# A two-layer audio trunk on one core: the last convolution block moved in front of the first scores, two casts moved behind key and query 1, and the norm weights' load moved to another queue

## The chip, the cores and the metric

One core of one Trainium2 chip. The time is device microseconds of one execution of the whole program; the comparison is between the median of several executions of the kernel before and of the changed kernel.

## What is computed

```python
for i in range(DEPTH):                                   # DEPTH = 2, 512 tokens, width 1024
    h = h + 0.5 * swiglu(rmsnorm(h, ffn1_norm[i]), ffn1_w_gu[i], ffn1_w_down[i])
    u = rmsnorm(h, mix_norm[i])
    b_g, c_g, v_c, q_c, kv_c, k_r, g_conv, g_mla = jnp.split(u @ w_in[i], split_pts, axis=-1)
    y_conv = short_conv_branch(b_g, c_g, v_c, conv_w[i], w_conv_out[i])
    y_mla = mla_branch(q_c, kv_c, k_r, q_norm[i], kv_norm[i], w_uq[i], w_ukv[i], w_mla_out[i], cos, sin)
    h = h + (sigmoid(g_conv) * y_conv + sigmoid(g_mla) * y_mla) @ w_o[i]
    h = h + 0.5 * swiglu(rmsnorm(h, ffn2_norm[i]), ffn2_w_gu[i], ffn2_w_down[i])
    h = h + sigmoid(rmsnorm(h, ple_norm[i]) @ w_ple_gate[i]) * (p[i] @ w_ple_proj[i])
return rmsnorm(h, final_norm)
```

`mla_branch` is attention with 8 heads. The queries of a head are 128 plain dimensions plus 64 that are turned by the token's position (rotary), keys likewise with one turned key shared by all heads; the mask is causal by chunks of 64 tokens.

## The kernel before

Everything is held transposed: a tile is 128 features by 512 tokens. All products are made in a 32-bit format of TensorE (fp32r) that keeps fewer bits, so every operand is cut into a high and a low part: ScalarE writes the high part (`split`: a copy with a cast, L204; for weights L70), VectorE the rest (a subtraction, L205; for weights L71), and a product of two operands is three matmuls, high times high, high times low, low times high (`mm3`, L212 to L214). Names that end in h and l are these parts.

Weights arrive in "halves" of eight 128 x 128 tiles, one DMA of 512 KB each on SyncE's queue, in the order in which the code asks for them (`Stream.get`). The cut weights `wh`, `wl` lie in 4 buffers each; a fifth cut can only start when the matmuls that read one of the four are done. TensorE's results go to a pool of 8 PSUM banks (`PS`): a new result needs a bank whose last reader is done.

The order of instructions on each engine is set when the program is built, by a scheduler that looks at the code's order and at its own estimates. Each engine then works through its list strictly in that order; an instruction that waits holds up all behind it on that engine.

The change lies in `mixer(l)`, which runs once per layer, and in the load of `cols`, the table of all norm weights. The stages of `mixer` that matter:

- The gates: products of seven parts each (`Sevens.step`, L427, 24 matmuls each); between them stand the blocks of the convolution's output, `conv_out(m)` for m = 0 to 7, each 12 matmuls of 512 columns, and one VectorE product with a gate (L650), which frees its bank. Nothing reads these products before the merge at the mixer's end.
- `qkv(pr)` for the four pairs of heads pr = 0 to 3: the turned queries of both heads (`q_rope`, bank `qr`), then `key(0)`, `query(0)`, `key(1)`, `query(1)` (banks `kn`, `qn`) and `values` (two banks `v`), each with its own cast into two parts; where `values` stands among them depends on how the weights fall into halves. `q_rope_parts` makes from the turned query (rope: `qrt`) one tile for each head (`qr0`, `qr1` below: ScalarE L701, VectorE L702), which the last two matmuls of each score block read.
- `scores(pr, t, ...)` for the heads t = 0, 1 of the pair: four blocks `s<pr><t>p`, one for each 128 queries, of 5 matmuls each over 256, 256, 384 and 512 keys; then VectorE's maximum (L741) and ScalarE's exponential (L743). `turn` transposes them (`t<pr><t>t`, cast into `pth`, `ptl`), and `mix_v` multiplies by the values (`o<pr><t>av`).
- The loop: `qkv(0)`, scores of both heads of pair 0, then for each pair `qkv` of the next, and twice: turn a head of this pair, scores of a head of the next, `mix_v`.

So the names `m0s10p` or `m0h1v` are: layer 0, pair 1, head 0, score block; layer 0, pair 1, values.

Of the kernel before, what the change touches and what calls it, by code (L numbers as in the profile page):

```python
# [9 lines left out]
F32 = mybir.dt.float32  # L10
F32R = mybir.dt.float32r
I32 = mybir.dt.int32
AF = mybir.ActivationFunctionType
ALU = mybir.AluOpType
# [158 lines left out]
def trunk_kernel(ctx, tc, dims, x, p, positions, gains, rope_c, weights, out):  # L173

    nc = tc.nc
    S, D, DEPTH, PD, DFF, CONV, QL, KL = dims
    KD = D // P
# [12 lines left out]
    def G(name, dt=F32):  # L190
        return gp.tile([P, S], dt, tag="g", name=name)

    def PS(name):
        return mp.tile([P, 512], F32, tag="mm", name=name)


    def split(src, name, scale=None):
        hi, lo = G(name + "h", F32R), G(name + "l", F32R)
        split_to(hi, lo, src, scale)
        return hi, lo  # L200

    def split_to(hi, lo, src, scale=None):
        if scale is None:
            nc.scalar.copy(hi, src)  # L204
            nc.vector.tensor_tensor(lo, src, hi.bitcast(F32), ALU.subtract)  # L205
        else:
            nc.scalar.activation(hi, src, AF.Copy, scale=scale)
            nc.vector.scalar_tensor_tensor(lo, src, scale, hi.bitcast(F32), ALU.mult, ALU.subtract)
# [7 lines left out]
    def proj(tiles, vs, name, ps=None):  # L216
        ps = PS(name) if ps is None else ps
        o = ps[:, :vs[0][0].shape[1]]
        for k, (t, v) in enumerate(zip(tiles, vs)):
            mm3(o, W.get(t), v, k == 0, k == len(tiles) - 1)  # L220
        return ps
# [19 lines left out]
    ones = cp.tile([P, P], F32R, tag="ones", name="ones")  # L241
    nc.vector.memset(ones.bitcast(F32), 1.0)
    cols = cp.tile([P, gains.shape[1]], F32, tag="cols", name="cols")
    nc.gpsimd.dma_start(out=cols, in_=gains)
    ident = cp.tile([P, P], F32, tag="ident", name="ident")
    make_identity(nc, ident)
    eps_t = cp.tile([P, 1], F32, tag="eps", name="eps_t")
# [301 lines left out]
    def rope(src, cos, sin, name):  # L549

        t1, t2 = G(name + "t1"), G(name + "t2")
        for a in range(0, P, 64):
            for o, i in ((a, a + 32), (a + 32, a)):
                nc.scalar.copy(t2[o:o + 32, :], src[i:i + 32, :])
        nc.vector.tensor_tensor(t1, src, cos, ALU.mult)
        nc.vector.tensor_tensor(t2, t2, sin, ALU.mult)
        nc.vector.tensor_tensor(t1, t1, t2, ALU.add)
        return t1

    def mixer(l):  # L560
# [32 lines left out]
        for k, (vh, vl) in enumerate(xs):  # L593
            if k % 4 == 0:
                wa, wb = W.halves_of(*kr_cols[k:k + 4])
            t = slice(k % 4 * P, (k % 4 + 1) * P)
# [18 lines left out]
        for k in range(CONV // P):  # L615
            ps = proj(W.col("w_in", l, o_c + k * P, D), xs, f"{name}Cp{k}")
            c = G(f"{name}c{k}")
            nc.vector.tensor_tensor(c, ps, r2, ALU.mult)
            ps = proj(W.col("w_in", l, o_v + k * P, D), xs, f"{name}Vp{k}")
# [7 lines left out]
            ps = proj(W.col("w_in", l, o_b + k * P, D), xs, f"{name}Bp{k}")  # L627
# [20 lines left out]
        def conv_out(m):  # L648
            ps = proj(W.col("w_conv_out", l, m * P, CONV), yc, f"{name}cop{m}")
            nc.vector.tensor_tensor(gates[m], ps, gates[m], ALU.mult)  # L650
# [4 lines left out]
            step(0, j)  # L655
        n_last = KD // 2 - 1
        for n in range(n_last):
            between = [(lambda m=m: conv_out(m)) for m in range(4 * n - 4, 4 * n)] if n else []
            order = [(n + 1, 1), (n, 7), (n + 1, 5), (n, 4)]
            order += [(n + 1, j) for j in ((6, 2, 7, 3, 4) if n + 1 == n_last else (2, 6, 3))]  # L660
            for i, (n_, j_) in enumerate(order):
                step(n_, j_)
                if i in (1, 2, 3, 4 if n + 1 == n_last else 5) and between:
                    between.pop(0)()
                if (n_, j_) == (n_last, 7):
                    qc = [split(t, f"{name}qn{k}") for k, t in enumerate(qt)]
                    kvc = [split(t, f"{name}kvn{k}") for k, t in enumerate(kvt)]
                    krh, krl = split(krt, name + "kr")
# [3 lines left out]
        def qkv(pr):  # L672
            n = f"{name}h{pr}"
            heads = (2 * pr, 2 * pr + 1)
            res = {}
            def values():
                vw = [W.get(*(("w_ukv", l, k * P, hd * 256 + NOPE) for hd in heads)) for k in range(KL // P)]
                vs = []
                for tb in range(0, NT, 2):
                    ps = PS(f"{n}v{tb}")  # L680
                    for b in range(2):
                        tok = slice((tb + b) * P, (tb + b + 1) * P)
                        o = ps[:, b * 256:(b + 1) * 256]
                        for k, (vh, vl) in enumerate(vw):
                            ch, cl = kvc[k][0][:, tok], kvc[k][1][:, tok]
                            nc.tensor.matmul(o, ch, vh, start=k == 0, stop=False)
                            nc.tensor.matmul(o, ch, vl, start=False, stop=False)
                            nc.tensor.matmul(o, cl, vh, start=False, stop=k == len(vw) - 1)
                    vs.append(split(ps, f"{n}v{tb}"))
                res["v"] = vs  # L690

            def q_rope():
                ps = proj(W.col("w_uq", l, tuple(hd * (NOPE + ROPE) + NOPE for hd in heads), QL), qc, n + "qr")
                res["qr"] = rope(ps, cosT, sinT, n + "qr")

            def q_rope_parts():
                qr = res["qr"]
                for t in range(2):
                    q2 = G(f"{n}qr{t}", F32R)
                    own, oth = slice(t * 64, t * 64 + 64), slice(64 - t * 64, 128 - t * 64)  # L700
                    nc.scalar.copy(q2[own, :], qr[own, :])  # L701
                    nc.vector.tensor_tensor(q2[oth, :], qr[own, :], q2[own, :].bitcast(F32), ALU.subtract)  # L702
                    res["qr", t] = q2

            def key(t):
                ps = proj(W.col("w_ukv", l, heads[t] * 256, KL), kvc, f"{n}kn{t}")
                res["kn", t] = split(ps, f"{n}kn{t}")

            def query(t):
                ps = proj(W.col("w_uq", l, heads[t] * (NOPE + ROPE), QL), qc, f"{n}qn{t}")  # L710
                res["qn", t] = split(ps, f"{n}qn{t}")

            query0 = lambda: query(0)
            parts = [(3, q_rope), (2, lambda: key(0)), (3, query0), (2, lambda: key(1)), (3, lambda: query(1))]
            at = [i for i in range(1, len(parts) + 1) if W.pairs_fit(2, sum(w for w, _ in parts[:i]))]
            parts.insert(at[-1], (4, values))
            for _, part in parts:
                part()
                if part is query0:
                    q_rope_parts()  # L720
            return res

        def scores(pr, t, qk):
            n = f"{name}s{pr}{t}"
            e = [G(f"{n}e{i}") for i in range(3)]
            e = [e[0][:, :P], e[1][:, :2 * P], e[0][:, P:], e[2]]
            sm = ep.tile([P, 16], F32, tag="sm", name=n + "sm")
            (qh, ql), (kh, kl), q2 = qk["qn", t], qk["kn", t], qk["qr", t]
            for i in range(NT):
                q = slice(i * P, (i + 1) * P)  # L730
                n_ = max(2, i + 1) * P
                ps = PS(f"{n}p{i}")
                o = ps[:, :n_]
                nc.tensor.matmul(o, qh[:, q], kh[:, :n_], start=True, stop=False)
                nc.tensor.matmul(o, qh[:, q], kl[:, :n_], start=False, stop=False)
                nc.tensor.matmul(o, ql[:, q], kh[:, :n_], start=False, stop=False)
                nc.tensor.matmul(o, q2[:, q], krh[:, :n_], start=False, stop=False)
                nc.tensor.matmul(o, q2[:, q], krl[:, :n_], start=False, stop=True)
                w = (i + 1) * P
                nc.vector.memset(ps[0:CHUNK, w - CHUNK:w], -1e30)  # L740
                nc.vector.tensor_reduce(sm[:, i:i + 1], ps[:, :w], axis=AX.X, op=ALU.max, negate=True)  # L741
                eo = e[i]
                nc.scalar.activation(eo, ps[:, :w], AF.Exp, bias=sm[:, i:i + 1], accum_out=sm[:, 8 + i:9 + i])  # L743
                nc.vector.reciprocal(sm[:, 12 + i:13 + i], sm[:, 8 + i:9 + i])
                (nc.vector if i % 2 else nc.gpsimd).tensor_scalar(eo, eo, sm[:, 12 + i:13 + i], None, ALU.mult)
            return e
# [31 lines left out]
        pt_h, pt_l = turned_tiles(name)  # L778
        heads = []
        qk = qkv(0)  # L780
        es = [scores(0, t, qk) for t in range(2)]
        NP = N_HEADS // 2
        for pr in range(NP):
# [12 lines left out]
        for m in range(KD):  # L796
            mla_part(m, N_HEADS - 2 if m < 3 else 0, N_HEADS)
            t = m_b[m]
# [3 lines left out]
        for m in range(KD):  # L802
            ps = proj(W.col("w_o", l, m * P, D), merged, f"{name}wop{m}")
# [206 lines left out]
```

## Time and profile before

| | us |
|---|---|
| three timed executions | 2289.72, 2289.80, 2291.17 (median 2289.8) |
| the profiled execution | 2290.97 |
| its span, first to last instruction | 2289.1 |
| TensorE busy in it | 2276.7 (99%) |
| VectorE, ScalarE, GpSimd busy | 1796.1, 1161.2, 34.7 |

Times in the rows of the timeline count from the span's start. A row of it has the start, the duration, the engine (an engine's name with a q is its queue, which issues DMAs), the line, the operation, what it writes and reads, shapes, and in brackets how long the engine sat idle before it and what ended that. Matmuls overlap: the distance between the starts of two is what one costs. Layer 1 repeats layer 0 in every stage spoken of here: its score stretches have the same lengths to 0.02 us.

### The profile page before, as it was taken

The page shows a single profiled execution, that of the slowest core. Times are in us where ns is not written, and L with a number is a line of the kernel's source. Part 1 is how long each engine was busy: PE and PEld are TensorE (multiplying, and loading weights), DVE is VectorE, ACT ScalarE, POOL GpSimd, SP SyncE. Part 2 cuts the span into 40 slices and gives each one's busy share as a digit, 9 for nine tenths or more (in the row PEclk, how much of TensorE's full clock was granted, in tenths as well). Part 3 has the DMA queues.
Part 4 walks back from the last instruction along what each step waited for, and adds up shares of the span by engine and source line. Part 5 has one row for each costly group of instructions (what it writes and reads, how often), then busy time and mean ns, then how long its engine had stood idle before and what let it go on. Part 6 is the DMA issues. An engine that isn't in the chain of part 4 may idle for free.

```text
span 2289.1 us, 34697 instructions
## 1 busy us (share of the span) xinstructions
PE 2276.7 (99%) x14168; PEld 2060.7 (90%) x14168; DVE 1796.1 (78%) x2508; ACT 1161.2 (51%) x1744; POOL 34.7 (2%) x43
## 2 busy tenths in 40 slices
PE   9999999999999999999999999999999999999998
PEld 8999988899888999998899999888988889999988
DVE  8887778877876988877798887768878669877765
ACT  7444445455743644444664444445467356444455
POOL 0000000000200000000000000000001000000000
PEclk9999999999999999999999999999999999999999
DMA  5333343134122233233223333322331123333321
GB/s 194 111 111 93 105 130 102 56 110 138 38 65 85 73 111 111 93 119 122 91 83 94 110 98 115 120 90 67 119 104 56 65 74 102 104 100 99 113 83 38
DMA packets 62975, 222.76 MB, mean 97 GB/s; under 512 B 7120, under 2 KB 7120, under 8 KB 62816
## 3 DMA queue, kind: packets, MB, share of 16 engines
q1 hardware_dynamic: 62208, 219.70, 30.4%
q8 instruction: 111, 1.82, 0.3%
q10 hardware_dynamic: 576, 0.79, 0.1%
q14 instruction: 48, 0.39, 0.1%
q0 software_dynamic: 32, 0.05, 0.0%
HBM read 218.42 MB, written 2.10 MB: 96 GB/s over the span
## 4 chain that ended last, share of the span: by engine, by line
PE 97%; DVE 2%; ACT 0%; issue 0%; DMA 0%; ACTq 0%; POOLq 0%
PE a0pd L212 2%; PE b0pd L212 2%; PE a1pd L212 2%; PE b1pd L212 2%; PE b1pd L213 2%; PE a1pd L213 2%; PE b0pd L213 2%; PE a0pd L213 2%; PE b1pd L214 2%; PE a1pd L214 2%; PE a0pd L214 2%; PE b0pd L214 2%; PE e1gp L212 1%; PE e1gp L214 1%; PE e1gp L213 1%; PE m0mop L212 1%
## 5 line engine op out<-in xcount | busy, mean ns | idle before, releaser
L70 ACT CAST wh<-st 128x1024 fp32r<-128x1024 f32 (+1 forms) x455 | 474.7, 1044 | 574.8 <-issue 57.7
L71 DVE TENSOR_TENSOR wl<-st,wh 128x1024 fp32r<-128x1024 f32 (+1 forms) x456 | 552.4, 1212 | 160.3 <-ACT wh L70 159.5
L70 ACT CAST wh<-s 128x1024 fp32r<-128x1024 f32 x94 | 98.8, 1051 | 132.6 <-PE b1pd L213 8.5
L71 DVE TENSOR_TENSOR wl<-s,wh 128x1024 fp32r<-128x1024 f32 x94 | 114.5, 1218 | 15.6 <-ACT wh L70 15.6
L149 DVE TENSOR_TENSOR st<-st,s 128x1024 f32<-128x1024 f32 x47 | 57.5, 1223 | 1.1
L146 DVE TENSOR_TENSOR s<-s,st 128x1024 f32<-128x1024 f32 x47 | 57.3, 1220 | 0.2
L141 DVE TENSOR_TENSOR s<-st,st 128x1024 f32<-128x1024 f32 x47 | 57.3, 1218 | 0.1
L152 DVE TENSOR_TENSOR st<-st,st 128x1024 f32<-128x1024 f32 x47 | 57.2, 1218 | 0.0
L511 DVE SCALAR_TENSOR_TENSOR h<-b0pd,h 128x512 f32<-128x512 f32 x40 | 27.5, 689 | 9.4 <-PE b0pd L214 9.2
L511 DVE SCALAR_TENSOR_TENSOR h<-b1pd,h 128x512 f32<-128x512 f32 x40 | 27.5, 688 | 9.4 <-PE b1pd L214 9.2
L511 DVE SCALAR_TENSOR_TENSOR h<-a1pd,h 128x512 f32<-128x512 f32 x40 | 27.5, 688 | 7.7 <-PE a1pd L214 7.7
L511 DVE SCALAR_TENSOR_TENSOR h<-a0pd,h 128x512 f32<-128x512 f32 x40 | 27.5, 687 | 6.4 <-PE a0pd L214 6.4
L106 POOL MEMSET wh<- 128x256 f32 x4 | 1.1, 313 | 1191.5 <-DVE wl L71 1191.5
L799 DVE TENSOR_TENSOR m1g<-m1mop,m1g 128x512 f32<-128x512 f32 x8 | 5.5, 690 | 6.5 <-PE m1mop L214 6.5
L799 DVE TENSOR_TENSOR m0g<-m0mop,m0g 128x512 f32<-128x512 f32 x8 | 5.5, 690 | 6.5 <-PE m0mop L214 6.5
L295 ACT ACT_TABLE_LOAD x8 | 10.3, 1283 | 0.1
L910 ACT ACTIVATE fsq<-h 128x256 f32<-128x256 f32 (+1 forms) x10 | 4.8, 480 | 9.9 <-DVE h L891 9.9
L804 DVE TENSOR_TENSOR h<-m0wop,h 128x512 f32<-128x512 f32 x8 | 5.5, 691 | 4.1 <-PE m0wop L214 4.1
L804 DVE TENSOR_TENSOR h<-m1wop,h 128x512 f32<-128x512 f32 x8 | 5.5, 690 | 4.1 <-PE m1wop L214 4.1
L621 DVE TENSOR_TENSOR m0z<-m0Vp,m0c 128x512 f32<-128x512 f32 x4 | 2.8, 692 | 6.2 <-PE m0Vp L214 6.2
L621 DVE TENSOR_TENSOR m1z<-m1Vp,m1c 128x512 f32<-128x512 f32 x4 | 2.8, 691 | 6.2 <-PE m1Vp L214 6.2
L650 DVE TENSOR_TENSOR m0g<-m0cop,m0g 128x512 f32<-128x512 f32 x8 | 5.5, 688 | 2.5 <-PE m0cop L214 2.5
(11171 smaller groups left out, 8787.5 us busy)
## 6 DMA issues: line engine op xcount, KB each, us to landing
st<-in_weights SPq DMA_DIRECT2D x406, 512.0 KB, 3.5
h<-in_x SPq DMA_DIRECT2D x8, 256.0 KB, 5.4
st<-in_weights SPq DMA_DIRECT2D x7, 256.0 KB, 5.3
out<-fo SPq DMA_DIRECT2D x7, 256.0 KB, 2.5
e0pi<-in_p SPq DMA_DIRECT2D x2, 256.0 KB, 3.7
e1pi<-in_p SPq DMA_DIRECT2D x2, 256.0 KB, 4.0
st<-in_weights ACTq DMA_DIRECT2D x1, 256.0 KB, 3.7
pos_i<-in_positions ACTq DMA_DIRECT2D x1, 256.0 KB, 3.8
```

The lines of the kernel that those rows point to most:

```text
L70: self.nc.scalar.copy(hi[:, w], src[:, w])
L71: self.nc.vector.tensor_tensor(lo[:, w], src[:, w], hi[:, w].bitcast(F32), ALU.subtract)
L141: tt(self.s, self.a21, self.a22, ALU.add)
L146: tt(self.s, self.s, self.a11, ALU.subtract)
L149: tt(self.a12, self.a12, self.s, ALU.subtract)
L152: tt(self.a11, self.a11, self.a21, ALU.subtract)
L212: nc.tensor.matmul(ps, wh, vh, start=first, stop=False)
L213: nc.tensor.matmul(ps, wh, vl, start=False, stop=False)
L214: nc.tensor.matmul(ps, wl, vh, start=False, stop=last)
L511: nc.vector.scalar_tensor_tensor(h[m], ps, 0.5, h[m], ALU.mult, ALU.add)
L799: nc.vector.tensor_tensor(t, mla_ps[m], t, ALU.mult)
L804: nc.vector.tensor_tensor(h[m], ps, h[m], ALU.add)
```

## The change

Three edits. The load of `cols` is issued by SyncE, as the first entry of its queue, and no longer by GpSimd. In `mixer`, `conv_out(7)` is no longer made between two steps of the gates, but after `qkv(0)` and ahead of the first scores. In `qkv`, `q_rope_parts` for both heads and the casts of the values come after all other parts, in that order.

```diff
-    nc.gpsimd.dma_start(out=cols, in_=gains)
+    nc.sync.dma_start(out=cols, in_=gains)
...
-            between = [(lambda m=m: conv_out(m)) for m in range(4 * n - 4, 4 * n)] if n else []
+            between = [(lambda m=m: conv_out(m)) for m in range(4 * n - 4, min(4 * n, KD - 1))] if n else []
...
-                    vs.append(split(ps, f"{n}v{tb}"))
+                    vs.append(ps)
                 res["v"] = vs
...
-            query0 = lambda: query(0)
-            parts = [(3, q_rope), (2, lambda: key(0)), (3, query0), (2, lambda: key(1)), (3, lambda: query(1))]
+            parts = [(3, q_rope), (2, lambda: key(0)), (3, lambda: query(0)), (2, lambda: key(1)), (3, lambda: query(1))]
             at = [i for i in range(1, len(parts) + 1) if W.pairs_fit(2, sum(w for w, _ in parts[:i]))]
             parts.insert(at[-1], (4, values))
             for _, part in parts:
                 part()
-                if part is query0:
-                    q_rope_parts()
+            for t in range(2):
+                q_rope_parts(t)
+            res["v"] = [split(ps, f"{n}v{2 * i}") for i, ps in enumerate(res["v"])]
             return res
...
         qk = qkv(0)
+        conv_out(KD - 1)
         es = [scores(0, t, qk) for t in range(2)]
```

`q_rope_parts(t)` now makes the tile of one head; its two instructions are unchanged (now L700 and L701).

What this does to the engines' lists. First pair, VectorE, from the first key's low part to the first maximum. Before:

```order
L205 TENSOR_TENSOR m0h0kn0l<-m0h0kn_5506,m0h0kn0h 128x512
L205 TENSOR_TENSOR m0h0qn0l<-m0h0qn_5517,m0h0qn0h 128x512
L71 TENSOR_TENSOR wl_6036<-st_6033,wh_6035 128x1024
L702 TENSOR_TENSOR m0h0qr_5531<-m0h0qrt_5497,m0h0qr_5531 64x512
L702 TENSOR_TENSOR m0h0qr_5534<-m0h0qrt_5497,m0h0qr_5534 64x512
L205 TENSOR_TENSOR m0h0kn1l<-m0h0kn_5537,m0h0kn1h 128x512
L205 TENSOR_TENSOR m0h0v0l<-m0h0v_5554,m0h0v0h 128x512
L205 TENSOR_TENSOR m0h0v2l<-m0h0v_5571,m0h0v2h 128x512
L205 TENSOR_TENSOR m0h0qn1l<-m0h0qn_5588,m0h0qn1h 128x512
L740 MEMSET m0s00p_5612 64x64
```

and in the changed kernel:

```order
L205 TENSOR_TENSOR m0h0kn0l<-m0h0kn_5486,m0h0kn0h 128x512
L205 TENSOR_TENSOR m0h0qn0l<-m0h0qn_5503,m0h0qn0h 128x512
L205 TENSOR_TENSOR m0h0kn1l<-m0h0kn_5517,m0h0kn1h 128x512
L205 TENSOR_TENSOR m0h0qn1l<-m0h0qn_5528,m0h0qn1h 128x512
L650 TENSOR_TENSOR m0g_4842<-m0cop_5588,m0g_4842 128x512
L71 TENSOR_TENSOR wl_6036<-st_6033,wh_6035 128x1024
L701 TENSOR_TENSOR m0h0qr_5574<-m0h0qrt_5477,m0h0qr_5574 64x512
L701 TENSOR_TENSOR m0h0qr_5577<-m0h0qrt_5477,m0h0qr_5577 64x512
L205 TENSOR_TENSOR m0h0v0l<-m0h0v_5548,m0h0v0h 128x512
L205 TENSOR_TENSOR m0h0v2l<-m0h0v_5561,m0h0v2h 128x512
L739 MEMSET m0s00p_5612 64x64
```

Key and query 1 moved up past a weight cut and the turned query; the moved block's gate product (L650) is new here. On TensorE the 12 matmuls of `conv_out(7)` now stand between the values and the first score block.

Second pair, ScalarE. Before:

```order
L701 CAST m0h1qr_5754<-m0h1qrt_5714 64x512
L701 CAST m0h1qr_5757<-m0h1qrt_5714 64x512
L204 CAST m0h1kn1h<-m0h1kn_5760 128x512
L70 CAST wh_6327<-st_6325 128x1024
L204 CAST m0h1qn1h<-m0h1qn_5771 128x512
```

and in the changed kernel:

```order
L204 CAST m0h1kn1h<-m0h1kn_5754 128x512
L204 CAST m0h1qn1h<-m0h1qn_5765 128x512
L70 CAST wh_6327<-st_6325 128x1024
L700 CAST m0h1qr_5811<-m0h1qrt_5714 64x512
L700 CAST m0h1qr_5814<-m0h1qrt_5714 64x512
L204 CAST m0h1v0h<-m0h1v_5785 128x512
```

The cut of the next weights (L70) stood behind the turned query's parts and now stands ahead of them; VectorE's list has the same order (its L71 for these weights directly ahead of L701).

Third pair, ScalarE; here `values` stand ahead of `query(1)`. Before:

```order
L701 CAST m0h2qr_6049<-m0h2qrt_6009 64x512
L701 CAST m0h2qr_6052<-m0h2qrt_6009 64x512
L204 CAST m0h2kn1h<-m0h2kn_6055 128x512
L70 CAST wh_6626<-st_6624 128x1024
L204 CAST m0h2v0h<-m0h2v_6066 128x512
L204 CAST m0h2v2h<-m0h2v_6083 128x512
L204 CAST m0pth_5473<-m0t10t_6120 128x512
L204 CAST m0h2qn1h<-m0h2qn_6100 128x512
```

and in the changed kernel:

```order
L204 CAST m0h2kn1h<-m0h2kn_6049 128x512
L70 CAST wh_6626<-st_6624 128x1024
L204 CAST m0h2qn1h<-m0h2qn_6086 128x512
L204 CAST m0pth_5459<-m0t10t_6120 128x512
L700 CAST m0h2qr_6106<-m0h2qrt_6009 64x512
L700 CAST m0h2qr_6109<-m0h2qrt_6009 64x512
L204 CAST m0h2v0h<-m0h2v_6060 128x512
```

The turned query's parts and the values' casts moved behind query 1 and behind the first transposed block (`pth`).

The banks follow the lists. In the first pair the score blocks take, in turn, the banks of `qr`, `kn0`, `qn0`, `kn1`, `qn1`, of the moved convolution block and of the two `v`; the next pair's `qr` takes that of the first score block. In the second pair the blocks of `s10` take those of `kn1`, `qn1` and the two `v`, before and after. In the third pair they took those of `kn1`, the two `v` and the first transposed block; now those of `kn1`, `qn1`, the first transposed block and the first `v`.

More of the change, by code (lines that the diff above doesn't have):

```diff
@@ L694, in q_rope, with q_rope_parts @@
                 res["qr"] = rope(ps, cosT, sinT, n + "qr")
-            def q_rope_parts():
+            def q_rope_parts(t):
                 qr = res["qr"]
[L698 to L703, printed above, removed]
+                q2 = G(f"{n}qr{t}", F32R)
+                own, oth = slice(t * 64, t * 64 + 64), slice(64 - t * 64, 128 - t * 64)
+                nc.scalar.copy(q2[own, :], qr[own, :])
+                nc.vector.tensor_tensor(q2[oth, :], qr[own, :], q2[own, :].bitcast(F32), ALU.subtract)
+                res["qr", t] = q2
             def key(t):
```

## The prediction

> **What bounds it now.** I read the page's busy times and chain first.
>
> ```profile
> PE 2276.7 (99%) x14168; PEld 2060.7 (90%) x14168; DVE 1796.1 (78%) x2508; ACT 1161.2 (51%) x1744; POOL 34.7 (2%) x43
> PE 97%; DVE 2%; ACT 0%; issue 0%; DMA 0%; ACTq 0%; POOLq 0%
> ```
>
> TensorE is the bound almost everywhere: of the span of 2289.1 us it is idle for 2289.1 - 2276.7 = 12.4. The change removes no matmul, so it can only move time in which TensorE waits. Where those waits are, the view of waits (TensorE's own) says: who waited, for whom, total, times, longest.
>
> ```profile
> PE a0pg L230 <- ACT a0x0h L207: 1.6, 1, 1.6
> PE m0s10p L734 <- DVE m0h1qn1l L205: 0.9, 1, 0.9
> PE m1s10p L734 <- DVE m1h1qn1l L205: 0.9, 1, 0.9
> ```
>
> One wait is at the start, and one in each layer in the scores of the second pair. Waits shorter than a matmul's own overlap are missed by this list, so I measured the score stages by windows of TensorE: from the first score matmul to the first matmul after the stage. The columns are the stretch, its length, TensorE's busy time, its granted clock, DMA share and GB/s. Both heads of pair 0; then head 0 of pair 1, of pair 2, head 1 of pair 2, head 0 of pair 3.
>
> ```profile
> 566.61:574.76 8.15, 7.84 (x41) 1.00 0.41 131
> 587.72:592.26 4.54, 3.67 (x21) 1.00 0.38 115
> 613.57:616.88 3.31, 3.31 (x24) 1.00 0.54 163
> 619.84:623.14 3.30, 3.30 (x24) 1.00 0.00 0
> 637.84:641.13 3.29, 3.29 (x23) 1.00 0.52 159
> ```
>
> A head that waits for nothing costs 3.29. Its 20 matmuls have 5 x (256 + 256 + 384 + 512) = 7040 columns, 0.467 ns each, so 0.12 us for a matmul of 256 columns, 0.18 for 384, 0.24 for 512. The first pair loses 8.15 - 2 x 3.29 = 1.57, the second pair's first head 4.54 - 3.29 = 1.25, the third and fourth pair nothing. Two layers: 2 x (1.57 + 1.25) = 5.6 us is all that the mixer edits can win.
>
> **The norm weights' queue.** The timeline's first microseconds, and from the DMA view the one issue of `h` at 0.73 with its time to landing:
>
> ```profile
> 0.73 0.38 SPq L53 DMA_DIRECT2D h<-in_x  x1
> 1.16 0.42 SPq L51 DMA_DIRECT2D st<-in_weights  x1
> 1.24 0.71 POOL L244 DMA_DIRECT2D cols<-in_gains  x1 [0.81 <-POOLq L999]
> 4.44 0.43 DVE L68 CAST wh<-st 128x512 fp32r<-128x512 f32 x1 [3.44 <-DMA st<-in_weights]
> 5.62 0.72 ACT L207 ACTIVATE a0x0h<-h,cols 128x512 fp32r<-128x512 f32 x1 [2.96 <-DMA cols<-in_gains]
> 6.40 0.80 PE L230 MATMUL a0pg<-a0x0h,wh 128*128 128x512 f32 x1 [1.57 <-ACT a0x0h L207]
> h<-in_x SPq DMA_DIRECT2D x1, 256.0 KB, 3.5
> 8.70 0.63 PE L232 MATMUL a0pu<-a0x0h,wl 128*128 128x512 f32 x1
> 9.12 0.53 PE L232 MATMUL a0pg<-a0x0h,wl 128*128 128x512 f32 x1
> 9.49 0.39 PE L232 MATMUL a0pu<-a0x0h,wl 128*128 128x512 f32 x1
> 9.71 0.39 PE L234 MATMUL a0pg<-a0x0l,wh 128*128 128x512 f32 x1
> ```
>
> ScalarE's first cast waits for `cols`, landed at 5.6, while `h` landed at 0.73 + 3.5 = 4.2. With `cols` first on SyncE, `h` takes the slot at 1.16, 0.43 later, and lands at about 4.7; every later issue of SyncE moves back by as much. No row shows 53 KB on this queue; 256 KB took 3.5, so I take `cols` as landed by 0.73 + 3.5 = 4.2. The cast then starts at 4.7 instead of 5.6, and the first product at about 5.5: 0.9 earlier. Bounds: nothing won, if `h` comes as late as `cols` did, and 1.4 (5.6 - 4.2), if the extra entry costs `h` nothing. The weights are ready (VectorE's cast ends at 4.87). The other tiles of x and weights may land 0.43 later, but the first tile keeps TensorE busy for 12 products of 0.22 to 0.42, so they are not missed. What 0.9 is worth depends on the clock: products start 0.42 apart up to 9.12 and 0.22 apart from 9.49 on, half speed at first. If the step stays at that moment, the 0.9 is won at half speed, 0.45; if it comes earlier with the work, 0.9. I take 0.7. GpSimd loses a DMA that nothing else of the start needs. The scheduler also swaps some neighbours in layer 0's first feed-forward; the wait list has nothing there, so I take 0.
>
> [...]
>
> **The first pair.** Rows of TensorE, ScalarE and VectorE:
>
> ```profile
> 554.79 0.40 PE L212 MATMUL m0h0qr<-m0qn0h,wh 128*128 128x512 f32 x1
> 559.77 0.73 ACT L646 ACTIVATE m0g<-m0g3t 128x256 f32<-128x256 f32 x2 [2.58 <-DVE m0g3t L641]
> 560.52 2.35 ACT L554 COPY m0h0qrt<-m0h0qr 32x512 f32<-32x512 f32 x4
> 565.84 0.68 DVE L205 TENSOR_TENSOR m0h0kn0l<-m0h0kn,m0h0kn0h 128x512 fp32r<-128x512 f32 x1
> 566.44 0.68 DVE L205 TENSOR_TENSOR m0h0qn0l<-m0h0qn,m0h0qn0h 128x512 fp32r<-128x512 f32 x1
> 567.04 1.23 DVE L71 TENSOR_TENSOR wl<-st,wh 128x1024 fp32r<-128x1024 f32 x1
> 568.29 1.40 DVE L702 TENSOR_TENSOR m0h0qr<-m0h0qrt,m0h0qr 64x512 fp32r<-64x512 f32 x2
> 572.21 0.19 DVE L740 MEMSET m0s00p<- 64x64 f32 x2
> 572.73 1.28 ACT L743 ACT_TABLE_LOAD   x1 [2.49 <-DVE m0s00sm L741]
> 574.02 0.37 ACT L743 ACTIVATE m0s00e<-m0s00p,m0s00sm 128x128 f32<-128x128 f32 x1
> ```
>
> A low part costs VectorE 0.60, a weight cut about 1.2, the two turned tiles 1.40. The convolution block, 12 x 0.23 = 2.8 of TensorE, is only moved: the gates' end comes 2.8 sooner, and the scores start when they did. What it gives is time for the casts. The casts themselves also move. The half that `conv_out(6)` opened now serves `q_rope` and key 0's first tile, so the weight cut that needs its buffer waits for the 12th product after the gates, 554.79 + 12 x 0.23 = 557.6 on the old time line (on which the scores would now start 2.7 later, at 569.3). Behind that cut (1.05, and 1.2 on VectorE) stand the turned key's low part 0.6, the last gate's product 0.7 and sigmoids 0.73, and the four copies for the turned query, 2.35: these end near 564.3, where they ended at 562.9. VectorE follows with three operations of the rotation (1.8), a cut (1.2), four low parts (2.4) and the convolution's product (0.6): 570.3, which is 1.0 after the scores' start, called zero from here. The next weight cut waits for the convolution block's third tile of four (its buffer) and is through ScalarE at 0.6, so VectorE does it next, to 2.2; the turned tiles are ready at 2.9 and 3.6, the values at 4.9. TensorE's first 18 matmuls (head 0 whole, two blocks of head 1, without turned tiles) need 2.7, so it waits some 0.2 for the first turned tile and would be through at 6.9. The next product, pair 1's `qr`, needs the bank of score block 0: maximum from 4.9, table load 0.52 after it as in the rows, exponential 1.29 after that, 0.37 long, and its read-out: 7.2. So 7.2 instead of 8.15, a gain of 0.95 per layer. Bounds: 0, and 1.57.
>
> **The second pair.**
>
> ```profile
> 583.62 0.28 PE L686 MATMUL m0h1v<-wh,m0kvn0h 128*128 128x256 f32 x1
> 586.34 1.05 ACT L70 CAST wh<-st 128x1024 fp32r<-128x1024 f32 x1
> 587.58 1.22 DVE L71 TENSOR_TENSOR wl<-st,wh 128x1024 fp32r<-128x1024 f32 x1
> 588.71 0.68 DVE L205 TENSOR_TENSOR m0h1qn1l<-m0h1qn,m0h1qn1h 128x512 fp32r<-128x512 f32 x1
> ```
>
> Count from the values' first matmul, V. Before, score block 0 starts at V + 4.1 and block 1 waits for its bank, that of query 1, whose low part stands behind the weight cut: to V + 5.8 (the wait of 0.9). That wait goes: query 1's low part is now ahead of the cut. What is late next is the cut itself: its buffer is read by the values' products to their end, V + 2.7 (586.34), on both engines, and the turned query now stands behind it. ScalarE's cut ends at V + 3.8, VectorE's 1.1 later at V + 4.9, the first turned tile at V + 5.6, the second at 6.3, the first value at 7.1. TensorE has six matmuls without them (0.7), stands at V + 4.9 until 5.7, does four (0.5), stands at 6.2 until the first value frees the bank of block 2 at 7.1, and needs 0.9 + 1.2 more: V + 9.2. Before it was 592.26 - 583.62 = 8.64. A loss of 0.55; bounds: a gain of 1.25, and a loss of 1.5 (both stands doubled).
>
> **The third pair**, whose values come ahead of query 1:
>
> ```profile
> 610.69 1.06 ACT L70 CAST wh<-st 128x1024 fp32r<-128x1024 f32 x1 [0.26 <-PE m0h2v L688]
> 612.57 0.49 PE L753 MATMUL m0t10t<-ident,m0s10e 128*128 128x128 f32 x3
> 613.68 0.59 ACT L204 CAST m0h2qn1h<-m0h2qn 128x512 fp32r<-128x512 f32 x1
> 616.40 0.18 DVE L740 MEMSET m0s20p<- 64x64 f32 x2
> ```
>
> Count from Q = 612.57, where query 1 is done; the scores start at Q + 1.0 and now lose nothing. After the change both turned tiles and both values wait behind query 1 in both lists. ScalarE: query 1 from Q + 0.2, first transposed block (0.6), turned tiles 0.6 each, done at 1.8 and 2.4. VectorE: query 1 at Q + 1.5, transposed block 2.1, turned tiles 2.8 and 3.5, first value 4.2. TensorE: nine matmuls without turned tiles (1.3), waiting 0.3 for banks, then for the turned tile to Q + 2.9; six more, 0.9; then block 3 needs the first value's bank, Q + 4.3, and 1.2: Q + 5.5 instead of 4.3. A loss of 1.2. Behind it VectorE reaches the maxima 2.2 late (Q + 6.0 for 3.8), TensorE only 1.2: block 1 of head 1 needs the bank of head 0's block 2, whose exponential is late by the difference less its slack: another 0.5. Bounds: 0, and 2.2 (all of VectorE's delay).
>
> **The fourth pair** again has query 1 ahead of the values, so query 1 is done 24 x 0.12 + 1.0 = 3.9 before the scores and not 1.0; by the same count the first value's low part ends about 0.6 before block 2 wants its bank: 0.
>
> **The sum.** A layer: -0.95 + 0.55 + 1.2 + 0.5 = +1.3; two layers +2.6; the start -0.7: +1.9. On the profiled execution's 2290.97 that is 2292.9. That execution lies 1.2 above the median of the runs, 2289.8; on the median it is 2291.7, a change of 0.08%. A change below 0.2% (4.6 us) is about what a measurement of this kernel cannot tell from none.
>
> **Rivals.**
> - [...] Chance 0.15.
> - The casts behind cost nothing: the cover holds in the first pair and later pairs stay as they were. 2289.8 - 2 x 0.95 - 0.7 = 2287.2. For it: VectorE idles in parts of every pair. Chance 0.21.
> - All score waits go: 2289.8 - 5.6 - 0.9 = 2283.3, faster. Against it: the cut that waits for the values stands ahead. Chance 0.05.
> - The backlog reaches the fourth pair too, where it pays like the third (1.7): 2291.7 + 2 x 1.7 = 2295.1, slower. It decides when the first value's low part of pair 3 ends over 0.6 later than my count, behind block 2's start. Chance 0.06.
> - The load does not come sooner, `h` queued behind small rows of `cols`: 2291.7 + 0.7 = 2292.4. Chance 0.04.
>
> My own forecast keeps 0.49, with 2290 to 2293.5 from the halved and full value of the start and half the spread of the pairs' bounds. The range, 2287.0 to 2294.2, takes in all but the two ends, 0.11, and some tail of the others. Faster 0.05, same 0.88, slower 0.07.
>
> **What would show it.** Right: the first product near 5.5; both first heads in about 7.2; the wait for query 1 in the second pair gone and replaced by two stands of about 0.9 before a matmul that reads `qr` and before one that reuses a value's bank; head 0 of pair 2 at 4.5 instead of 3.3. Wrong: if that last stretch is still 3.3, or if pair 3's is not. A start that does not move would show ScalarE's first cast waiting for `h` near 5.6.

## The result, and the profile after

The changed kernel takes 2295.01 us in the median of 16 executions (2291.69 to 2295.49), the kernel before 2290.55 beside it (16 executions, 2289.67 to 2292.67). The ratio is 1.0016, with a 95% interval of 1.0008 to 1.0023. That is slower, by less than the 0.2% that the prediction called no change, and above the upper end of its range, 2294.2.

The executions of the changed kernel fall into three groups: two at 2291.7 to 2291.9, five at 2293.3 to 2293.6, nine at 2294.9 to 2295.5, some 1.7 apart. The profiled execution, 2291.93 with a span of 2289.9, is one of the first group, so its trace shows less than what the median lost. Its busy times differ little from before:

```profile
PE 2275.3 (99%) x14168; PEld 2059.0 (90%) x14168; DVE 1798.5 (79%) x2508; ACT 1161.3 (51%) x1744; POOL 33.1 (1%) x42
```

TensorE now idles 2289.9 - 2275.3 = 14.6 us where it idled 12.4. Its waits (total, times, longest):

```profile
PE a0pg L230 <- ACT a0x0h L207: 1.4, 1, 1.4
PE m0s10p L736 <- DVE m0h1qr L701: 1.0, 1, 1.0
PE m0s10p L733 <- DVE m0h1v0l L205: 0.8, 1, 0.8
PE m0s20p L733 <- DVE m0h2v0l L205: 0.3, 1, 0.3
```

The wait for query 1 is gone; in its place stand one for the turned query and one for the bank that the first value holds, and the third pair has got a wait. The score stretches that the prediction measured, in the same order (stretch, length, TensorE busy, granted clock, DMA share, GB/s):

```profile
564.35:571.47 7.12, 6.87 (x41) 1.00 0.25 94
584.33:589.89 5.56, 3.81 (x23) 1.00 0.30 94
611.20:615.77 4.57, 4.22 (x23) 1.00 0.38 118
618.71:622.36 3.65, 3.64 (x23) 1.00 0.00 0
637.06:640.41 3.35, 3.35 (x23) 1.00 0.36 135
```

Against 8.15, 4.54, 3.31, 3.30 and 3.29: -1.03, +1.02, +1.26, +0.35, +0.06. The whole loss of a layer can be read from its first score to a product far behind; first the row of before, then that of the changed kernel:

```profile
805.10 0.40 PE L212 MATMUL b0pd<-b0a0h,wh 128*128 128x512 f32 x1
```

```profile
804.38 0.40 PE L212 MATMUL b0pd<-b0a0h,wh 128*128 128x512 f32 x1
```

805.10 - 566.61 = 238.49, 804.38 - 564.35 = 240.03: 1.54 lost in each layer, 3.1 in both. At the start, the two loads have changed places, and `h` ends the wait of ScalarE's first cast:

```profile
0.72 0.39 SPq L244 DMA_DIRECT2D cols<-in_gains  x1
1.16 0.42 SPq L53 DMA_DIRECT2D h<-in_x  x1
5.11 0.72 ACT L207 ACTIVATE a0x0h<-h,cols 128x512 fp32r<-128x512 f32 x1 [2.45 <-DMA h<-in_x]
5.88 0.50 PE L230 MATMUL a0pg<-a0x0h,wh 128*128 128x512 f32 x1 [1.41 <-ACT a0x0h L207]
```

So every wait that the prediction named is there, and none of them explains the third group of executions. Two theories for it, both on the clock that TensorE is granted (at 0.50, in the repeated run below, products of 512 columns start 0.42 apart instead of 0.23): A, the two stands of the second pair lie so close that the clock falls to half behind them, in some executions; B, the clock steps up later at the start than it did.

### The profile page after: what moved, and what is told of

Same layout as the page of the kernel before. It is cut to its first block, busy times and chain, and to the rows that moved or that the text cites. A ratio compares the mean times of both kernels' runs of the same rounds, so it can differ in the third digit from the quotient of the medians.

```text
span 2289.9 us, 34697 instructions
## 1 busy us (share of the span) xinstructions
PE 2275.3 (99%) x14168; PEld 2059.0 (90%) x14168; DVE 1798.5 (79%) x2508; ACT 1161.3 (51%) x1744; POOL 33.1 (1%) x42
## 4 chain that ended last, share of the span: by engine, by line
PE 96%; DVE 2%; ACT 1%; issue 0%; DMA 0%; SPq 0%; ACTq 0%
PE b0pd L212 2%; PE b1pd L212 2%; PE a0pd L212 2%; PE a1pd L212 2%; PE a1pd L213 2%; PE a0pd L213 2%; PE b1pd L213 2%; PE b0pd L213 2%; PE b0pd L214 2%; PE a1pd L214 2%; PE b1pd L214 2%; PE a0pd L214 2%; PE e1gp L212 1%; PE e1gp L214 1%; PE e1gp L213 1%; PE m0mop L212 1%
## 5 line engine op out<-in xcount | busy, mean ns | idle before, releaser
L70 ACT CAST wh<-st 128x1024 fp32r<-128x1024 f32 (+1 forms) x455 | 474.7, 1044 | 576.0 <-issue 58.2
L71 DVE TENSOR_TENSOR wl<-st,wh 128x1024 fp32r<-128x1024 f32 (+1 forms) x456 | 552.8, 1213 | 162.0 <-ACT wh L70 161.0
L70 ACT CAST wh<-s 128x1024 fp32r<-128x1024 f32 x94 | 98.8, 1051 | 130.9 <-PE a1pd L213 8.5
L71 DVE TENSOR_TENSOR wl<-s,wh 128x1024 fp32r<-128x1024 f32 x94 | 114.6, 1219 | 14.1 <-ACT wh L70 14.1
```

Of the source, the lines that this page charges most:

```text
L70: self.nc.scalar.copy(hi[:, w], src[:, w])
L71: self.nc.vector.tensor_tensor(lo[:, w], src[:, w], hi[:, w].bitcast(F32), ALU.subtract)
```

## The experiments

Each ratio below is to the kernel before, executed beside the run; its median there was 2289.8 to 2291.3.

**The changed kernel again**, profiled anew, no edit.

> The changed kernel once more, for the spread of its times and for the clock in a second profile. Its profile so far shows waits that cost each layer 1.54 us, 3.1 in all, and a start 2.3 us quicker than in the profile of before; yet its times mostly lie 4 to 5.5 above before's lower times (2289.8). Theory A (the stands drop the clock): in most executions the two stands of 0.95 and 0.8 us in the second pair let the clock fall to half for some microseconds, once per layer, 1.7 us each; then times lie near 2291.8, 2293.5 and 2295.3, and a profile of a 2293.5 or 2295.3 execution shows a granted clock below 1 near 587 or 1720 us. Theory B (the start): the clock steps up later at the start in most executions; such a profile shows the step near 7.4 or 10.8 us and a full clock afterwards. Both expect a median of 2293.5 to 2295.5.

2293.72 (2291.85 to 2295.55), ratio 1.0013 (1.0004 to 1.0022). This profile is of an execution of the third group, 2294.75. Its windows of TensorE (second column length, third busy, then the granted clock), and its timeline at the place:

```profile
586.28:589.69 3.41, 1.67 (x11) 1.00 0.49 148
589.69:593.10 3.41, 3.41 (x11) 0.50 0.04 11
```

```profile
587.62 0.39 PE L736 MATMUL m0s10p<-m0krh,m0h1qr 128*128 128x256 f32 x1 [0.95 <-DVE m0h1qr L701]
589.15 0.41 PE L733 MATMUL m0s10p<-m0h1kn0h,m0h1qn0h 128*128 128x384 f32 x1 [0.79 <-DVE m0h1v0l L205]
590.43 0.63 PE L733 MATMUL m0s10p<-m0h1kn0h,m0h1qn0h 128*128 128x512 f32 x1
590.85 0.63 PE L734 MATMUL m0s10p<-m0h1kn0l,m0h1qn0h 128*128 128x512 f32 x1
```

The clock is 0.50 for 3.41 us, and matmuls of 512 columns start 0.42 apart instead of 0.23. The window ahead of it holds both stands and is busy for 1.67 of 3.41, 49%. By this pitch half of 3.41, 1.7, is the most that such a window costs, an estimate; read from the first score to the product far behind, it cost 1.53, since this layer takes 807.28 - 565.72 = 241.56 where the first group's execution took 240.03:

```profile
565.72 0.28 PE L733 MATMUL m0s00p<-m0h0kn0h,m0h0qn0h 128*128 128x256 f32 x1
807.28 0.40 PE L212 MATMUL b0pd<-b0a0h,wh 128*128 128x512 f32 x1
```

The fall is only half of what parts the two executions (2294.75 - 2291.93 = 2.82). The other half is the start: by the traces' record of the granted clock it steps up at 9.43 here and at 3.97 there, and the first score comes at 565.72 instead of 564.35, 1.37 later. The kernel before has executions with a late step too (9.40 in its profile), so this half is no loss against it.

From the clock's step up at 9.43 to this fall are 580.26 us, 170 times 3.4133. From the step up to the fall at the program's end are 2282.68 - 9.40 = 2273.28 in the profile of before and 2284.08 - 3.97 = 2280.11 in that of the first group, 666 and 668 times the same length. So in these three traces the changes of the clock lie whole windows of 3.4133 apart. In the profiled execution of the first group, with its step up at 3.97, windows counted in the same way (3.97 + 170 x 3.4133 = 584.24) cut off the end of the second stand, and the clock stays up (0.50 stands in no window of that stage):

```profile
584.24:587.65 3.41, 1.78 (x14) 1.00 0.29 72
```

Theory A, then, though this is only a coincidence until the idleness is taken away.

**The stands filled.** Products with a tile of zeros, in the second pair's first scores:

```diff
+                if pr == 1 and t == 0 and i == 0:
+                    for _ in range(6):
+                        nc.tensor.matmul(o, zero, kh[:, :n_], start=False, stop=False)
                 nc.tensor.matmul(o, q2[:, q], krh[:, :n_], start=False, stop=False)
+                if pr == 1 and t == 0 and i == 1:
+                    for _ in range(5):
+                        nc.tensor.matmul(o, zero, kh[:, :n_], start=False, stop=False)
```

> The changed kernel, with products of a tile of zeros added into the second pair's first scores: six 128x256 products ahead of the first product that waits for the turned query (6 x 0.12 us = 0.72 us, in a stand of 0.95 us) and five ahead of the last product of the second block (0.60 us, in a stand of 0.8 us). Nothing is computed otherwise and nothing comes sooner; TensorE only has work in the two stands. Theory A (two stands close together inside one window let the clock fall to half for the next window): the score block still takes about 5.6 us to the first product of the mix, but no window at half clock stands behind it in the profile, and the times lose their upper part: groups near 2291.9 and 2293.6, none at 2294.6 to 2295.5, median 2292 to 2293.6, so 1 to 2 us below the changed kernel. Theory C (the fall of the clock, or the time above what the waits explain, hangs on the moved casts in another way, not on TensorE's idleness): times as the changed kernel's, median 2293.7 to 2295, with the upper group still there.

2293.34 (2291.62 to 2293.62), ratio 1.0008 (0.9999 to 1.0017). None of the 11 executions lies above 2293.62, where 14 of the 27 of the changed kernel were above 2294.5. Nothing came sooner: the second pair still takes 5.54 to the mix, of which TensorE is now busy 5.08. In its layer 1 the windows, counted as above from its step up (5.12), hold both stands whole, as in the execution that lost its clock, and the next window runs at full clock:

```profile
584.28:589.82 5.54, 5.08 (x34) 1.00 0.26 95
1718.61:1722.02 3.41, 2.97 (x21) 1.00 0.43 154
1722.02:1725.44 3.42, 3.42 (x21) 1.00 0.03 5
```

The granted clock of each whole execution, on record to three digits, says the same: in the changed kernel it is 0.999 in the five executions below 2293 and 0.998 in the other 22, with the stands filled it is 0.999 in all eleven. So the middle group of the changed kernel seems to hold a fall as well, with an early step up at the start. This is a weak sign, since the half clock behind the last products counts in that digit too, and no profile of that group was taken.

Eleven useless products that nothing waits for, and the upper group is gone: Theory A is shown, and C falls. What is left, 2291.6 to 2292.0 and 2292.8 to 2293.6, lies some 2.2 above the two groups of the kernel before (from 2289.4 and from 2290.8): the waits' 3.1 less the start's 0.9.

**Old casts in the second pair alone.** `values` and `q_rope_parts` at their old places for `pr == 1`.

> The whole change, except that the second pair (and it alone) keeps the old places of its casts. Theory A: the two stands of the second pair go, its score block is 4.5 us to the mix as before, no window at half clock; the third pair's waits (4.57 us where 3.31 stood, and 0.35 us behind) stay. From the kernel with old casts in pairs 1 to 3 (groups at 2286.8 and 2288.9) plus 2 x 1.6 us: groups near 2290.0 and 2292.1, median 2290 to 2292. Theory C (the third pair's wait or the last block's new place makes the excess): an upper group at 2293 or above stays.

2290.97 (2290.61 to 2292.61), ratio 1.0002 (0.9994 to 1.0011): two groups, 2290.6 to 2291.0 and 2292.2 to 2292.6, near those forecast. The second pair is back at 4.52 and the third still waits:

```profile
584.91:589.43 4.52, 3.64 (x20) 1.00 0.40 116
610.75:615.32 4.57, 4.22 (x23) 1.00 0.38 118
```

**The old casts in pairs 1 to 3**, the rest changed.

> The whole change, but the casts are moved behind key and query 1 in the first pair alone; pairs 1 to 3 keep the order of before. The waits of pairs 1 and 2 that the change brought should go and the first pair's gain of about 0.9 per layer stay: 1.8 less than before from the mixer. Theory A: the clock does not fall, the start gives 0.5 to 1: 2287.0 to 2288.5, faster than before. Theory B: the start costs as much as in the changed kernel: 2289.0 to 2291.

2288.69 (2286.80 to 2289.33), ratio 0.9988 (0.9979 to 0.9997). The first heads of the second and third pairs take 4.53 and 3.32, as before; this beats both kernels. The time lies between the ranges of the two theories, so the median alone does not decide; the next runs on the start do. What is left of the change is the start, the block, and the casts in the first pair.

**The mixer's edits without the load**, `cols` back on GpSimd's queue.

> Of the change, only the mixer's edits (convolution block and casts); the norm weights stay on GpSimd's queue. Theory A: all of the loss, 2293.5 to 2296.5, with times in steps of about 1.7. Theory B: only the 3.1 of the waits: 2292.9 to 2294.5, with the two groups of before.

2295.92 (2292.47 to 2296.95), ratio 1.0018 (1.0009 to 1.0027), as Theory A has it. Its profile, of an execution of 2296.16, has the half clock at the same place in the program, behind a window that is busy for 1.66:

```profile
587.37:590.78 3.41, 1.66 (x12) 1.00 0.30 106
590.78:594.19 3.41, 3.41 (x10) 0.50 0.12 48
```

**The load alone**, the first line of the diff.

> Of the change, only the norm weights' load on SyncE's queue. Theory A: the first product comes 0.5 earlier, the stages behind are as before: 2289.0 to 2291.0, equal to or below before by 0.5 to 1. Theory B: the clock steps up later in most executions: 2291.5 to 2293, above before.

2288.94 (2288.25 to 2290.61), ratio 0.9994 (0.9985 to 1.0003). The first product comes at 5.46 instead of 6.40, 0.94 sooner and not 0.5:

```profile
5.46 0.80 PE L230 MATMUL a0pg<-a0x0h,wh 128*128 128x512 f32 x1 [0.64 <-ACT a0x0h L207]
```

The kernel before, executed beside it, has two groups, from 2289.4 and from 2290.9; this one has them from 2288.25 and from 2289.9. Both moved down by about 1, so the start is won, not lost: against B. The interval alone would not settle it.

**The block alone**, the two lines on `conv_out`.

> The kernel before, with only the last convolution block moved; casts and norm weights stay. Theory 1 (the block alone gives the first pair's time): both heads of the first pair in 7.1 to 7.4 us instead of 8.15, the other pairs 4.5 and 3.3: 1.5 to 2 us below the kernel before in the same call, 2288.8 to 2289.5 in the median. Theory 2 (the casts' new place is what shortens the first pair, the block only moves): 7.9 to 8.2 us, and no difference to the kernel before (within 0.5 us). By the kernel with the values alone moved (6.47 us) a value as low as 6.5 to 6.8 would say that the turned query's late parts cost 0.7 us there as well.

2287.73 (2285.93 to 2289.07), ratio 0.9984 (0.9975 to 0.9992), better than expected of either theory:

```profile
567.04:573.51 6.47, 6.47 (x42) 1.00 0.04 16
586.30:590.82 4.52, 3.56 (x22) 1.00 0.30 103
```

The first pair takes 6.47, less than two heads that wait for nothing by the prediction's count (6.58), and the others are as before (4.52, and 3.30 for the first head of the third): 1.68 won in each layer, 3.4 in both. In the changed kernel the moved casts take 7.12 - 6.47 = 0.65 of it back.

**The casts alone**, the edits in `qkv`.

> The kernel before, with only the casts moved (turned query and values, in all pairs); the last convolution block and the norm weights stay. Theory S (the casts alone make the loss, whatever the block does): second pair's first head 5.5 to 5.6 us with the two stands, third pair 4.5 to 4.6 us and 3.6 to 3.7 behind it, first pair 8.1 to 9.0; two layers of 2.6 to 3.4 us, 5 to 7 us, and the window at half clock in most executions: median 2295.5 to 2299. Theory I (the loss comes from casts and block together, because the block's place shifts the buffers): second and third pair within 0.3 us of 4.5 and 3.3, median 2289 to 2292.

2296.08 (2295.95 to 2299.03), ratio 1.0029 (1.0018 to 1.0041), with four of seven executions at 2296.0 to 2296.1 and three up to 2299.03. The profiled execution is of the lower four, with no window at half clock in the mixer:

```profile
566.94:574.87 7.93, 7.60 (x41) 1.00 0.37 129
587.74:593.30 5.56, 3.81 (x24) 1.00 0.26 94
614.60:619.17 4.57, 4.22 (x24) 1.00 0.37 118
```

The casts win 0.22 in the first pair and lose in the second and third what they lose in the changed kernel, with or without the block: Theory S. From the first score to the product far behind, layer 0 takes 807.77 - 566.94 = 240.83 and layer 1 240.90, where both took 238.49: 2.34 and 2.41 lost, 4.75 in both, a little under the 5 to 7 expected. That most executions hold a window at half clock is not shown: the one profile has none, and none was taken of the upper three.

**One cast at a time**, with block and load moved. First the values' alone:

```diff
+                if part is query0:
+                    q_rope_parts(0)
+                    q_rope_parts(1)
-            for t in range(2):
-                q_rope_parts(t)
```

> The whole change, except that the turned query's parts are cast at their old place (right behind query 0) in all pairs; only the values' casts stay behind key and query 1. Theory A with the values' cast alone as a cause of the short second stand: in the second pair the wait for the turned query goes (0.95 us), a wait of 0.3 to 0.8 us for the bank that the values' cast frees stays, so its score block is 4.8 to 5.3 us; one stand leaves the clock up; third pair 3.3 to 4.6 us. Median 2287.5 to 2291.5, no group above 2292.5. Rival: the work on VectorE ahead of the scores is the same sum in another order, so that one stand of about 1.8 us takes the place of two: block at 5.5 us, the clock falls all the same, median 2293 to 2295.

2286.83 (2285.02 to 2287.03), ratio 0.9980 (0.9971 to 0.9989): below what was expected. The wait for the first value's bank stays, 1.0 us of it, but the second pair takes no longer for it than before, 4.52. Then the turned query's alone, the values cast at once:

```diff
-                    vs.append(ps)
+                    vs.append(split(ps, f"{n}v{tb}"))
...
-            res["v"] = [split(ps, f"{n}v{2 * i}") for i, ps in enumerate(res["v"])]
```

> The whole change with the values cast at their old place, at once behind their products; only the turned query's parts are cast behind key and query 1. Theory Q (the turned query's late parts make the waits of the changed kernel in the second and third pairs): first pair 7.1 to 7.5 us, second pair's first head 5.3 to 6.0 us with a wait for the turned query of 1.3 to 1.8, third pair 3.9 to 4.6; a long stand may also drop the clock: median 2291 to 2295. Theory V (the values' late casts make them): second and third pair 4.5 and 3.3 as before, median 2286.5 to 2289.

2287.37 (2285.88 to 2288.06), ratio 0.9982 (0.9973 to 0.9991). The first three score stretches of the one, and of the other:

```profile
566.09:572.56 6.47, 6.47 (x42) 1.00 0.06 22
585.62:590.14 4.52, 3.55 (x20) 1.00 0.35 112
611.46:614.76 3.30, 3.30 (x23) 1.00 0.50 159
```

```profile
566.36:573.06 6.70, 6.70 (x42) 1.00 0.04 17
585.79:589.74 3.95, 3.64 (x24) 1.00 0.39 122
611.53:615.07 3.54, 3.54 (x23) 1.00 0.46 153
```

Neither cast alone makes the loss; I had expected one of the two theories of the second kernel to hold, and both fell. It takes both: from the first score to the product far behind, layer 0 takes 236.61 with the block alone moved, 236.89 with the values' casts as well, 237.08 with the turned query's, and 240.03 with both. VectorE's timeline ahead of the third pair's scores shows why there, first with the values alone moved, then with both:

```profile
607.98 1.41 DVE L701 TENSOR_TENSOR m0h2qr<-m0h2qrt,m0h2qr 64x512 fp32r<-64x512 f32 x2
610.02 1.22 DVE L71 TENSOR_TENSOR wl<-st,wh 128x1024 fp32r<-128x1024 f32 x1
```

```profile
609.40 1.23 DVE L71 TENSOR_TENSOR wl<-st,wh 128x1024 fp32r<-128x1024 f32 x1 [1.46 <-ACT wh L70]
611.00 0.69 DVE L205 TENSOR_TENSOR m0h2qn1l<-m0h2qn,m0h2qn1h 128x512 fp32r<-128x512 f32 x1 [0.38 <-ACT m0h2qn1h L204]
612.32 1.41 DVE L701 TENSOR_TENSOR m0h2qr<-m0h2qrt,m0h2qr 64x512 fp32r<-64x512 f32 x2
613.76 0.69 DVE L205 TENSOR_TENSOR m0h2v0l<-m0h2v,m0h2v0h 128x512 fp32r<-128x512 f32 x1
```

With one group of casts left in place, VectorE works on it ahead of the weight cut (with the turned query's moved it is the values' low parts, from 608.54). With both behind, it stands idle for 1.46 + 0.38 and then has all of it to do while TensorE waits.

**The start's two groups.** The kernel with old casts in pairs 1 to 3, with `range(8)` of the idle products at L319 turned into `range(11)`; then the same on the kernel with the values alone moved.

> The kernel with the last convolution block moved, the norm weights on SyncE's queue and the casts moved in the first pair alone (2288.69, groups at 2286.8 to 2287.5 and 2288.5 to 2289.3), with 11 instead of 8 idle products ahead of the first real one, so that TensorE has no gap of 1 us there. Theory A' (the two groups are the clock stepping up one window sooner or later, by how busy the window ahead of the first product was): the lower group alone, 2286.8 to 2287.6. Theory B' (they come from the phase of the windows alone): both groups as before, median 2288 to 2289; or 0.3 to 0.7 us more if the idle products still run when the first block's norm is ready.

> The whole change with the turned query cast at its old place (2286.83, groups at 2285.0 to 2285.6 and 2286.8 to 2287.0), and 11 instead of 8 idle products ahead of the first real one. The two findings add up if the groups are the clock's step at the start: one group, 2285.0 to 2285.8. If the bridge only moved the phase of the windows in the other kernel, both groups stay and the median is 2286 to 2287.

2287.35 (2286.97 to 2287.88), ratio 0.9984 (0.9975 to 0.9993), and 2285.28 (2284.85 to 2285.57), ratio 0.9976 (0.9967 to 0.9986): one group each where there were two, and the second is the fastest kernel here. The idle products now reach to the first real one, which runs at full speed (0.31 to the next start, where it was 0.59 at half speed; timeline of the last kernel):

```profile
1.03 4.88 PE L320 MATMUL idle<-ones 128*128 128x128 f32 x22 [1.03 <-DVE hpi L250]
5.67 0.48 PE L230 MATMUL a0pg<-a0x0h,wh 128*128 128x512 f32 x1
5.98 0.40 PE L230 MATMUL a0pu<-a0x0h,wh 128*128 128x512 f32 x1
```

That the groups are the clock's step, sooner or later, fits both; the lower end of the range did not move, only the upper. The profiles agree: the clock steps up at 10.67 and 10.07 in the two kernels with 8 idle products (executions of the upper groups), at 5.90 and 5.59 in those with 11.

## Why the prediction was wrong

Its time, 2291.7, and its upper end, 2294.2, were too low. By its steps:

- **The start, -0.7.** Right, and a little more: the first product came at 5.46 in the kernel with the load alone (forecast: about 5.5), both groups of times fell by about 1, and of two executions whose clock stepped up at 9.4 the changed kernel's had its first score 566.61 - 565.72 = 0.89 sooner. In the changed kernel's first profile it came at 5.88, with the products behind it 0.23 apart: there the clock had stepped up before them. In the repeated one they ran at half speed until 9.4. So the step comes earlier in some executions and not in others.
- **The first pair, -0.95 a layer.** Measured -1.03. But the working took block and casts for one gain; the block alone wins 1.68, and the casts cost 0.65.
- **The second pair, +0.55.** Both stands are there, where they were counted: the turned query's until V + 5.79 (586.24 after the values' first matmul at 580.45; forecast 5.7), the value's bank until V + 7.32 (forecast 7.1). The mix starts at V + 9.44 (589.89) instead of the forecast 9.2, a loss of 0.80 against the 8.64 of before.
- **The third pair, +1.2 and +0.5 behind it.** +1.26 and +0.35. **The fourth, 0:** +0.06.
- **The sum of the waits, +2.6.** 3.1, mis-sized by 0.5, mostly in the second pair.

The rows behind the second pair's numbers, TensorE's from the changed kernel's first profile:

```profile
580.45 0.28 PE L686 MATMUL m0h1v<-wh,m0kvn0h 128*128 128x256 f32 x1
586.24 0.39 PE L736 MATMUL m0s10p<-m0krh,m0h1qr 128*128 128x256 f32 x1 [0.95 <-DVE m0h1qr L701]
587.77 0.41 PE L733 MATMUL m0s10p<-m0h1kn0h,m0h1qn0h 128*128 128x384 f32 x1 [0.80 <-DVE m0h1v0l L205]
```

The step that failed is the price of these two stands. The prediction put each down at its own length and spoke of the clock only at the start. Two stands that each leave it up alone (the kernel before has one of 0.9, the kernel with the values alone moved one of 1.0, and no window at half clock in the mixer in their profiles) take 1.74 out of one window of 3.41 together, and the next window then runs at half speed: 1.5 more, in the executions whose windows lie so.

The account, between two executions whose clock stepped up at 9.4, that of before (2290.97) and the repeated one (2294.75): the start -0.9, the waits +3.1, the window at half clock +1.5, together +3.7; measured were 3.78. The prediction had 2292.9 for it, so of the 1.9 that it lacks the clock is 1.5 and the waits 0.5, and the start gives 0.2 back. The two medians lie further apart, 4.46, because before's falls between its two groups, eight executions in each, and the changed kernel's into its uppermost.

By the distance of the two layers, an execution of the changed kernel holds one such window at most, an estimate. In the repeated one, layer 1 has the first score of its second pair 1720.70 - 585.71 = 1134.99 behind layer 0, 332 windows and 1.76. The stands reach from 586.67 to 589.15, 2.48, which leaves a window 0.93 to hold both whole; windows that do so in layer 0 and cost 1.5 there cut those of layer 1 apart (there the window with the longer part of them, from 1719.50, is busy for 2.47, and the clock stays up). How many executions have one was read only from the third digit of the clock (22 of 27); of the four profiles of kernels with both stands two have it. The rival of the fourth pair gave 2295.1, near the time measured, but its mechanism isn't there: that the number is near is luck.

## What to carry to other kernels

On a TensorE that is nearly always busy, short waits are not priced one by one: here two stands that took 1.74 out of one window of 3.41 us cost another 1.5 by the clock, where single stands of 0.9 and 1.0 left it up. So add up the idle time of such a stretch, or fill the stands with products that nobody needs: here that left no execution above 2293.62, where 14 of 27 had been above 2294.5. Casts that one engine can do while it would wait for something else are best left there: moving one group of two cost 0.3 to 0.5 a layer, moving both 3.4, since it took away their cover. And an edit that bundles a gain (the block, 3.4, and the load, 1) with a loss (the casts, 4.75 in their own trace) is taken apart before it is judged.

## What the hardware showed that was not expected

The clock fell behind windows in which TensorE was busy for 1.66 and 1.67 of 3.41 us and stayed up behind one with 1.78. That does not make half of the busy time a limit: at the end of the kernel before it fell behind a window that was busy for 2.57.

```profile
2279.27:2282.68 3.41, 2.57 (x22) 1.00 0.32 123
2282.68:2286.10 3.42, 0.01 (x1) 0.50 0.40 149
```

From 2279.30 on this window holds only products of one column (`fss`) and transposes of 128 (`ft`). At the end of the changed kernel it fell behind a window of such work that was busy for 2.02, and behind one with 2.01 at the start, of idle products and of the first products of 512 columns, it stayed up:

```profile
3.97:7.39 3.42, 2.01 (x11) 1.00 0.93 313
2280.66:2284.08 3.42, 2.02 (x16) 1.00 0.05 19
2284.08:2287.49 3.41, 0.00 (x0) 0.50 0.57 213
```

What parts these windows is not shown.

At the start, with the windows placed by the later step, one that was busy for 2.80 did not raise the clock (the repeated run), nor did one with 2.25 (2.58 to 5.99 in the kernel before); one with 2.92 did (the kernel with old casts in the second pair), as did one with 2.94 (0.56 to 3.97 in the changed kernel's first profile) and one with 3.00 (5.99 to 9.40 in the kernel before). There the clock's column still reads 1.00, and only the pitch of the matmuls tells the half speed.

```profile
2.60:6.02 3.42, 2.80 (x12) 1.00 0.97 282
```

```profile
1.90:5.31 3.41, 2.92 (x14) 1.00 0.98 277
```
